# Low parts of a projection's weights by an accumulating DMA in place of a GpSimd subtraction

## The chip, the cores and the metric

The kernel runs on one core of one Trainium2 chip, as one launch. The metric is the device time of that launch in microseconds (us). A core has five engines that run their own instruction streams and wait for each other by semaphores: PE (TensorE, matmuls; its weight loads are listed as PEld), DVE (VectorE), ACT (ScalarE), POOL (GpSimd) and SP (SyncE, which here only issues DMAs). DMAs issued by SP and by POOL move data between HBM and SBUF, or within SBUF.

## The reference, cut to what matters

The reference is a two-layer decoder trunk on 512 tokens of width 1024, all in float32. The piece that the change touches is the first step of layer 1's attention (multi-head latent attention):

```python
def mla_mixer(x, w_down, q_norm, kv_norm, w_uq, w_ukv, w_out):
    down = x @ w_down                      # (512 x 1024) @ (1024 x 800)
    cq, ckv, kr = jnp.split(down, [512, 768], axis=-1)
    q = (rms_norm(cq, q_norm) @ w_uq).reshape(bsz, s, 16, 96)
    ...
```

Its input x is the output of layer 0: `x = layer_norm(DN_ALPHA * h + f + e, ln2_g, ln2_b)`, where f is the last product of layer 0's MLP. So the end of an MLP, a layer norm and this projection follow each other.

## The kernel before

Every matmul is made of three: each float32 operand is split into a high part of type fp32r (a copy with conversion) and a low part (the operand minus its high part), and the products high·high, high·low and low·high are summed in PSUM. `split` (L88) does this with a copy on ACT (L89) and a subtraction on DVE, or on POOL where `sub=nc.gpsimd.tensor_sub` is given (L90). `wload` (L92) loads a weight tile `wraw` with a DMA of SP's queue (L98) and splits it, in `pieces` column blocks, into `whi` and `wlo`. There are two buffers each of `wraw`, `whi` and `wlo` for the whole program, so the split of a tile waits until the matmuls of the tile before the last have read their buffer. A scheduler orders the instructions of each engine at build time; `ahead` raises the priority of a split in it.

Activations stand transposed: eight row tiles `y0` to `y7` of 128 features x 512 tokens. The stretch around the change has these steps:

- Layer 0's last MLP product adds its column tiles into `y4` to `y7` (DVE, L884). The last two, `y6` and `y7`, are made in two halves of 256 tokens (`tail=1`).
- The layer norm (class `Norm`, `onepass`) sums as the tiles come: DVE adds `y` into `n_s1` (L245), ACT squares `y` into `n_sq` (L256), DVE adds that into `n_s2` (L257). For each token half, PE then turns the sums into columns (L274), DVE and ACT make mean and inverse deviation (`n_m`, `n_d`; L277 to L283), PE spreads them (L288), and DVE and ACT make the scaled rows and their parts `hh` and `hl` (L318, L319, L327, L328). POOL makes `y` ready for the next residual (L330).
- PE's stream is in order, and the scheduler has put these small matmuls between those of other work: the first half's L274 stands among the MLP's last matmuls (L107 to L109), the second half's among those of the projection.
- `group_n` (L905) is the projection. Its weights are `w_dn0` (query, 512 columns) and `w_dn1` (key/value, 288 columns). Each has two weight tiles ("chunk 0" and "chunk 1" in what follows), and each chunk has four row tiles k, split one by one (`pieces=4`). For tokens 0 to 255 PE goes through k = 0 to 7 (L916 with `whi`, L917 with `wlo`, L918 with `hl`, for two token blocks each, so six matmuls for a k), then for tokens 256 to 511 again. So chunk 0 serves k = 0 to 3 and chunk 1 k = 4 to 7. The low parts of all of them are made on POOL.

Of the kernel before, what the change touches and what calls it, by code (L numbers as in the profile page):

```python
# [12 lines left out]
OP = mybir.AluOpType  # L13
# [40 lines left out]
def hybrid_kernel(ctx: ExitStack, tc: tile.TileContext, a: dict, out: bass.AP):  # L54
    nc = tc.nc
    uid = [0]

    def nm(s):
        uid[0] += 1
        return f"{s}_{uid[0]}"  # L60
# [9 lines left out]
    def f(ap):  # L70
        return ap.bitcast(F32)
# [7 lines left out]
    def ps_tile(tag=None):  # L79
        if tag is None:  # L80
            tag = TURN[turn[0] % 6]
            turn[0] += 1
        return psum.tile([P, S], F32, tag=tag, bufs=BANKS[tag], name=nm("ps"))
# [4 lines left out]
    def split(hi, lo, src, act=None, sub=None):  # L88
        (act or nc.scalar.copy)(hi, src)  # L89
        (sub or nc.vector.tensor_sub)(lo, src, f(hi))  # L90

    def wload(dram, idx, n=2048, pieces=2, sub=None, raw=None, ahead=30):  # L92

        hi = wp.tile([P, 2048], F32R, tag="whi", name=nm("whi"))
        lo = wp.tile([P, 2048], F32R, tag="wlo", name=nm("wlo"))
        if raw is None:
            raw = wp.tile([P, 2048], F32, tag="wraw", name=nm("wraw"))
            nc.sync.dma_start(raw[:, :n], dram[idx, :, :n])  # L98
        m = n // pieces
        with tc.high_priority(ahead):  # L100
            for i in range(pieces):
                c = slice(i * m, (i + 1) * m)
                split(hi[:, c], lo[:, c], raw[:, c], sub=sub)
        return hi, lo

    def mm3(ps, whi, wlo, xhi, xlo, start, stop):
        nc.tensor.matmul(ps, whi, xhi, start=start, stop=False)  # L107
        nc.tensor.matmul(ps, whi, xlo, start=False, stop=False)  # L108
        nc.tensor.matmul(ps, wlo, xhi, start=False, stop=stop)  # L109
# [1 line left out]
    ALL, HALVES = slice(0, S), (slice(0, H), slice(H, S))  # L111

    def gemm_t(dram, idxs, xs, evac, kk=8, nt=2, lead=0, ps=ps_tile, sub=None, loaded=None,
               halves=(), tail=0, ahead=30):

        tiles = {}  # L120

        def part(g, c, w, kn, cs=ALL):
            ktot = kk * len(idxs[g])
            for k, n in kn:
                key = g, n, cs.start
                if key not in tiles:
                    tiles[key] = ps()
                kx = c * kk + k
                hi, lo = xs[kx]
                o = slice((k * nt + n) * P, (k * nt + n + 1) * P)  # L130
                mm3(tiles[key][:, cs], w[0][:, o], w[1][:, o], hi[:, cs], lo[:, cs],
                    kx == 0, kx == ktot - 1)
                if kx == ktot - 1:
                    evac(g * nt + n, tiles[key], cs)

        first, last = 0, len(idxs) - tail
        byn = [(k, n) for n in range(nt) for k in range(kk)]
        byk = [(k, n) for k in range(kk) for n in range(nt)]
        if lead:
            w = loaded or [wload(dram, idxs[g][0], sub=sub, ahead=ahead) for g in range(2)]  # L140
            first = 2
            for cs in HALVES if "lead" in halves else (ALL,):
                for k in range(lead):
                    for g in range(2):
                        part(g, 0, w[g], [(k, n) for n in range(nt)], cs)
                for g in range(2):
                    kn = (byk, byn)[g]
                    part(g, 0, w[g], [t for t in kn if t[0] >= lead], cs)
        for g in range(first, last):
            for c, idx in enumerate(idxs[g]):  # L150
                part(g, c, wload(dram, idx, sub=sub, ahead=ahead), byn)
        if tail:
            w = {(g, c): wload(dram, idx, sub=sub, ahead=ahead) for g in range(last, len(idxs)) for c, idx in enumerate(idxs[g])}
            for cs in HALVES:
                for g in range(last, len(idxs)):
                    cn = [(c, n) for n in range(nt) for c in range(len(idxs[g]))]
                    for c, n in cn if cs.start == 0 else sorted(cn):
                        part(g, c, w[g, c], [(k, n) for k in range(kk)], cs)
# [12 lines left out]
    for k in range(KT):  # L171
        c = slice(k * 256, (k + 1) * 256)
# [283 lines left out]
    def mixer0(mixed):  # L456
        with pool("m0", 1) as m0, pool("m0s") as sc:
# [58 lines left out]

            kt = []
            gemm_t(a["w_in"], [[1], [0]], x, ev0, lead=8, loaded=w0)


# [139 lines left out]

            rcs = []
            gemm_t(a["w_in"], [[2], [3]], x, ev1, sub=nc.gpsimd.tensor_sub)
            topk()
            gemm_full([4, 5], ev2)
# [58 lines left out]
    def out_proj(dram, idxs, xs, norm, **kw):  # L723
        def ev(n, ps, cs):
            yn = y[n][:, cs]
            nc.vector.tensor_add(yn, yn, ps[:, cs])
            if n == 3:
                norm.first()
            elif n > 3:
                norm.add(n, cs)  # L730


        first = iter((ps_g, ps_g))
        gemm_t(dram, idxs, xs, ev, ps=lambda: next(first, ps_tile)(), **kw)
# [165 lines left out]
    def mixer1(x1, mixed):  # L900
        with pool("m1", 1) as m1, ExitStack() as pools:
            cst_ = ExitStack()
            cp = cst_.enter_context(pool("m1c"))

            def group_n(dram, ncols, xs, evac):  # L905

                ps = [ps_tile() for _ in range(NB)]
                w = [[u[:, :4 * ncols].rearrange("p (k n) -> p k n", n=ncols)
                      for u in wload(dram, ci, 4 * ncols, pieces=4, sub=nc.gpsimd.tensor_sub)] for ci in range(2)]
                for half in range(2):  # L910
                    for k in range(KT):
                        for b in (2 * half, 2 * half + 1):
                            c = slice(b * P, (b + 1) * P)
                            o = ps[b][:, :ncols]
                            (hi, lo), (whi, wlo) = xs[k], (u[:, k % 4] for u in w[k // 4])
                            nc.tensor.matmul(o, hi[:, c], whi, start=k == 0, stop=False)  # L916
                            nc.tensor.matmul(o, hi[:, c], wlo, start=False, stop=False)  # L917
                            nc.tensor.matmul(o, lo[:, c], whi, start=False, stop=k == KT - 1)  # L918
                    for b in (2 * half, 2 * half + 1):
                        evac(b, ps[b])  # L920
# [12 lines left out]
            def transposed(src, n, col, tag):  # L933

                o = []
                for i in range(n):
                    pt = ps_tile()
                    for b in range(NB):
                        nc.tensor.transpose(pt[:, b * P:(b + 1) * P], src[b][:, i * P:(i + 1) * P], ident)
                    g = small[:, col + i:col + i + 1]  # L940
                    hi = m1.tile([P, S], F32R, tag=f"{tag}h{i}", name=nm(tag))
                    lo = m1.tile([P, S], F32R, tag=f"{tag}l{i}", name=nm(tag))
                    nc.scalar.activation(hi, pt, AF.Copy, scale=g)
                    nc.vector.scalar_tensor_tensor(lo, pt, g, f(hi), op0=OP.mult, op1=OP.subtract)
                    o.append((hi, lo))
                return o
# [8 lines left out]
            def ev_kv(b, ps):  # L955
                ckn[b] = rms_scale(ps[:, :256], 256)
                nc.scalar.copy(kr[:, b], ps[:, 256:288])

            group_n(a["w_dn0"], 512, x1, ev_q)
            group_n(a["w_dn1"], 288, x1, ev_kv)  # L960
            cq = transposed(cqn, 4, C_QN, "cq")

            def rope(dst, src, tmp, cs, sn):
# [8 lines left out]
            for b in range(NB):  # L972
                ps = ps_tile()
                c = slice(b * P, (b + 1) * P)
                for k in range(4):
                    hi, lo = cq[k]
# [128 lines left out]
    for layer in range(2):  # L1105
        mixed = [None] * KT
        if layer == 0:
            mixer0(mixed)
        else:
            mixer1(h, mixed)  # L1110
        with pool(f"mlp{layer}") as mp:
            with pool(f"norm{layer}a", 1) as npool:
                norm = Norm(npool, layer, 0)
                if layer == 0:
                    out_proj(a["w_out0"], [[2], [3]], mixed[4:], norm, kk=4, nt=4, tail=1, sub=nc.gpsimd.tensor_sub)
                else:
                    out_proj(a["w_out1"], [[i] for i in range(4)], mixed, norm, lead=7, tail=2)
                pp = embed(layer, mp)
            h = mlp(layer, norm, pp, mp)
# [98 lines left out]
```

## Time and profile before

| | |
|---|---|
| median of 3 runs | 1269.17 us (1267.67 to 1270.79) |
| the profiled execution: its own time | 1267.45 us |
| its span (first to last instruction) | 1265.7 us |
| PE busy | 1225.8 us, 97% of the span |
| DVE busy | 924.4 us, 73% |
| ACT busy | 667.1 us, 53% |
| POOL busy | 167.4 us, 13% |
| mean granted TensorE clock | 0.99 of full speed |

The busy share of PE is that of pipelined matmuls whose ends are modelled, so a busy PE is not a PE at its peak; what counts is where it stood idle, for whom, and at which granted clock it ran. [...] Idle time of an engine that nobody waits for costs nothing. Times of rows are microseconds from the start of the span. One row of a merged view can stand for several instructions in a row (x3), and then its second number is the stretch that they filled together.

### The profile page before, as it was taken

The page shows a single profiled execution, that of the slowest core. Times are in us where ns is not written, and L with a number is a line of the kernel's source. Part 1 is how long each engine was busy: PE and PEld are TensorE (multiplying, and loading weights), DVE is VectorE, ACT ScalarE, POOL GpSimd, SP SyncE. Part 2 cuts the span into 40 slices and gives each one's busy share as a digit, 9 for nine tenths or more (in the row PEclk, how much of TensorE's full clock was granted, in tenths as well). Part 3 has the DMA queues.
Part 4 walks back from the last instruction along what each step waited for, and adds up shares of the span by engine and source line. Part 5 has one row for each costly group of instructions (what it writes and reads, how often), then busy time and mean ns, then how long its engine had stood idle before and what let it go on. Part 6 is the DMA issues. An engine that isn't in the chain of part 4 may idle for free.

```text
span 1265.7 us, 18749 instructions
## 1 busy us (share of the span) xinstructions
PE 1225.8 (97%) x7240; PEld 1063.4 (84%) x7240; DVE 924.4 (73%) x1793; ACT 667.1 (53%) x1216; POOL 167.4 (13%) x202
## 2 busy tenths in 40 slices
PE   8898899999999999999899999999999999999998
PEld 6744678989899898897797888799898998988987
DVE  5998867998566575586838788579985674855857
ACT  4594664656335254364356888446563362542633
POOL 0501660000000000000544553300000000000000
PEclk9998899999999999999999999999999999999999
DMA  6211122122323314123113111122232231231311
GB/s 217 101 33 67 67 76 75 68 101 100 126 75 134 100 67 134 67 101 133 38 68 117 51 51 51 50 85 83 100 134 97 70 133 68 100 134 67 134 34 68
DMA packets 22457, 113.07 MB, mean 89 GB/s; under 512 B 2976, under 2 KB 7072, under 8 KB 10176
## 3 DMA queue, kind: packets, MB, share of 16 engines
q1 hardware_dynamic: 22272, 111.28, 25.6%
q8 instruction: 57, 0.93, 0.3%
q0 software_dynamic: 96, 0.59, 0.2%
q14 instruction: 32, 0.26, 0.1%
HBM read 107.66 MB, written 2.10 MB: 87 GB/s over the span
## 4 chain that ended last, share of the span: by engine, by line
PE 81%; DVE 12%; ACT 3%; issue 1%; POOL 1%; DMA 1%; ACTq 0%; SPq 0%; POOLq 0%; DVEq 0%
PE ps L793 26%; PE ps L107 15%; PE ps L108 15%; PE ps L109 15%; DVE mb L551 2%; DVE m L550 2%; PE ps L397 2%; PE ps L417 1%; ACT whi L89 1%; PE ps L1095 1%; PE ps L917 1%; PE ps L918 1%; PE ps L916 1%; PE ps L1096 1%; DVE xc L611 1%
## 5 line engine op out<-in xcount | busy, mean ns | idle before, releaser
L89 ACT CAST whi<-wraw 128x1024 fp32r<-128x1024 f32 (+3 forms) x154 | 129.9, 882 | 151.2 <-PE ps L108 118.3
L107 PE MATMUL ps<-ah,whi 128*128 128x512 f32 (+1 forms) x544 | 206.4, 379 | 0.0
L108 PE MATMUL ps<-al,whi 128*128 128x512 f32 (+1 forms) x544 | 206.4, 379 | 0.0
L109 PE MATMUL ps<-ah,wlo 128*128 128x512 f32 (+1 forms) x544 | 205.3, 377 | 0.0
L107 PE MATMUL ps<-hh,whi 128*128 128x256 f32 (+1 forms) x432 | 147.1, 343 | 6.7 <-ACT hh L89 5.2
L109 PE MATMUL ps<-hh,wlo 128*128 128x256 f32 (+1 forms) x432 | 145.4, 340 | 1.4 <-DVE wlo L90 0.8
L108 PE MATMUL ps<-hl,whi 128*128 128x256 f32 (+1 forms) x432 | 146.5, 340 | 0.0
L90 POOL TENSOR_TENSOR wlo<-wraw,whi 128x512 fp32r<-128x512 f32 (+2 forms) x46 | 72.8, 1605 | 472.8 <-ACT whi L89 440.3
L90 DVE TENSOR_TENSOR wlo<-wraw,whi 128x1024 fp32r<-128x1024 f32 (+1 forms) x108 | 115.6, 1102 | 19.9 <-ACT whi L89 19.7
L793 PE MATMUL ps<-xt,whi 128*128 128x256 f32 x680 | 124.6, 284 | 0.0
L108 PEld LDWEIGHTS ps<-al,whi 128*128 128x128 f32 x544 | 102.8, 189 | 20.1 <-DVE al L90 1.2
L107 PEld LDWEIGHTS ps<-ah,whi 128*128 128x128 f32 x544 | 102.8, 189 | 19.5 <-ACT ah L89 1.1
L109 PEld LDWEIGHTS ps<-ah,wlo 128*128 128x128 f32 x544 | 102.8, 189 | 18.6 <-issue 0.5
L793 PEld LDWEIGHTS ps<-xt,whi 128*128 128x128 f32 x680 | 106.0, 192 | 0.4
L758 ACT CAST whi<-wraw 128x1024 fp32r<-128x1024 f32 (+1 forms) x43 | 36.0, 837 | 130.8 <-PE ps L108 89.6
L884 DVE TENSOR_TENSOR y<-y,ps 128x512 f32<-128x512 f32 (+1 forms) x52 | 33.3, 644 | 94.7 <-PE ps L109 94.6
L793 PE MATMUL ps<-xt,wlo 128*128 128x256 f32 x340 | 96.2, 283 | 0.0
L107 PEld LDWEIGHTS ps<-hh,whi 128*128 128x128 f32 x432 | 82.7, 192 | 16.1 <-ACT hh L89 5.2
L109 PEld LDWEIGHTS ps<-hh,wlo 128*128 128x128 f32 x432 | 82.5, 192 | 11.3 <-DVE wlo L90 2.0
L108 PEld LDWEIGHTS ps<-hl,whi 128*128 128x128 f32 x432 | 82.9, 192 | 8.7 <-DVE hl L90 0.6
L793 PE MATMUL ps<-hh,wlo 128*128 128x256 f32 x260 | 73.5, 283 | 0.0
L793 PE MATMUL ps<-hl,whi 128*128 128x256 f32 x260 | 73.5, 283 | 0.0
(335 smaller groups left out, 2951.7 us busy)
## 6 DMA issues: line engine op xcount, KB each, us to landing
wraw<-in_mlp_w SPq DMA_DIRECT2D x64, 1024.0 KB, 4.8
wraw<-in_w_out SPq DMA_DIRECT2D x8, 1024.0 KB, 5.1
wraw<-in_w_gate SPq DMA_DIRECT2D x8, 1024.0 KB, 4.7
wraw<-in_w_in SPq DMA_DIRECT2D x6, 1024.0 KB, 4.7
wraw<-in_w_ukv SPq DMA_DIRECT2D x4, 1024.0 KB, 4.7
wraw<-in_w_in SPq DMA_DIRECT2D x16, 128.0 KB, 5.0
y<-in_xT SPq DMA_DIRECT2D x8, 256.0 KB, 3.6
wraw<-in_w_proj SPq DMA_DIRECT2D x2, 1024.0 KB, 4.9
```

What stands on the lines that cost most here:

```text
L89: (act or nc.scalar.copy)(hi, src)
L90: (sub or nc.vector.tensor_sub)(lo, src, f(hi))
L107: nc.tensor.matmul(ps, whi, xhi, start=start, stop=False)
L108: nc.tensor.matmul(ps, whi, xlo, start=False, stop=False)
L109: nc.tensor.matmul(ps, wlo, xhi, start=False, stop=stop)
L397: nc.tensor.transpose(ps[t][:, c:c + P], self.L[blk][:, kb * P:(kb + 1) * P], ident)
L417: nc.tensor.matmul(po[:, c], v, hi, start=kb == 0, stop=kb == NB - 1)
L550: nc.vector.max(out=m8, in_=src)
L551: nc.vector.match_replace(out=w, in_to_replace=m8, in_values=src, imm_value=LOWEST)
L758: nc.scalar.copy(hi, src)
L793: nc.tensor.matmul(o, u[:, c], v, start=start and k == n == 0, stop=k == 3 and n == 2, skip_group_check=True)
L884: nc.vector.tensor_add(yn, yn, ps[:, cs])
```

## The change

For the query part `w_dn0` alone, the four pieces of both chunks are no longer split with a POOL subtraction. ACT copies the piece into `whi` as before, then ACT writes the negated high part into `wlo`, and a DMA issued from POOL's queue adds the raw weights to it in place (`accum_op`). The other weights keep their split; `w_dn1` gets its subtraction named in the call. The scheduler's priority step for these pieces is 60 in place of 30. Six lines come in ahead, so the lines of the kernel after are 6 higher from L107 on (L330 becomes L336, L917 becomes L923).

```diff
-    def wload(dram, idx, n=2048, pieces=2, sub=None, raw=None, ahead=30):
+    def wload(dram, idx, n=2048, pieces=2, sub=None, raw=None, ahead=30, adds=False):
...
         with tc.high_priority(ahead):
             for i in range(pieces):
                 c = slice(i * m, (i + 1) * m)
-                split(hi[:, c], lo[:, c], raw[:, c], sub=sub)
+                if adds:
+                    nc.scalar.copy(hi[:, c], raw[:, c])
+                    nc.scalar.mul(lo[:, c], f(hi[:, c]), -1.0)
+                    nc.gpsimd.dma_start(f(lo[:, c]), raw[:, c], accum_op=OP.add)
+                else:
+                    split(hi[:, c], lo[:, c], raw[:, c], sub=sub)
...
-            def group_n(dram, ncols, xs, evac):
+            def group_n(dram, ncols, xs, evac, **how):
...
-                      for u in wload(dram, ci, 4 * ncols, pieces=4, sub=nc.gpsimd.tensor_sub)] for ci in range(2)]
+                      for u in wload(dram, ci, 4 * ncols, pieces=4, **how)] for ci in range(2)]
...
-            group_n(a["w_dn0"], 512, x1, ev_q)
-            group_n(a["w_dn1"], 288, x1, ev_kv)
+            group_n(a["w_dn0"], 512, x1, ev_q, ahead=60, adds=True)
+            group_n(a["w_dn1"], 288, x1, ev_kv, sub=nc.gpsimd.tensor_sub)
```

POOL's order from the first piece of chunk 0 on, before (`wlo_5857` is chunk 0, `wlo_5869` chunk 1; `y_67` to `y_74` are `y0` to `y7`, first token half):

```order
L90 TENSOR_TENSOR wlo_5857<-wraw_5858,whi_5856 128x512 x4
L330 TENSOR_SCALAR y_67<-y_67,small 128x256
L330 TENSOR_SCALAR y_68<-y_68,small 128x256
L330 TENSOR_SCALAR y_69<-y_69,small 128x256
L90 TENSOR_TENSOR wlo_5869<-wraw_5870,whi_5868 128x512 x2
L330 TENSOR_SCALAR y_70<-y_70,small 128x256
L90 TENSOR_TENSOR wlo_5869<-wraw_5870,whi_5868 128x512
L330 TENSOR_SCALAR y_71<-y_71,small 128x256
L90 TENSOR_TENSOR wlo_5869<-wraw_5870,whi_5868 128x512
```

The same place in the change (`wlo_5873` is chunk 1 now):

```order
L107 DMA wlo_5857<-wraw_5858 128x512 x4
L336 TENSOR_SCALAR y_67<-y_67,small 128x256
L336 TENSOR_SCALAR y_68<-y_68,small 128x256
L336 TENSOR_SCALAR y_69<-y_69,small 128x256
L336 TENSOR_SCALAR y_70<-y_70,small 128x256
L107 DMA wlo_5873<-wraw_5874 128x512
L336 TENSOR_SCALAR y_71<-y_71,small 128x256
L107 DMA wlo_5873<-wraw_5874 128x512 x2
L336 TENSOR_SCALAR y_72<-y_72,small 128x256
L336 TENSOR_SCALAR y_73<-y_73,small 128x256
L107 DMA wlo_5873<-wraw_5874 128x512
```

The eight subtractions are gone, eight DMA issues stand in their place, and the first one of chunk 1 has moved behind the step on `y3` (`y_70`).

ACT's order at chunk 0, before (the squares are those of `y3` to `y6`):

```order
L256 ACTIVATE n_sq_5511<-y_70 128x512
L89 CAST whi_5856<-wraw_5858 128x512 x3
L256 ACTIVATE n_sq_5549<-y_71 128x512
L89 CAST whi_5856<-wraw_5858 128x512
L256 ACTIVATE n_sq_5579<-y_72 128x512
L256 ACTIVATE n_sq_5617<-y_73 128x256
```

And in the change:

```order
L262 ACTIVATE n_sq_5511<-y_70 128x512
L105 CAST whi_5856<-wraw_5858 128x512 x2
L106 ACTIVATE wlo_5857<-whi_5856 128x512
L262 ACTIVATE n_sq_5549<-y_71 128x512
L106 ACTIVATE wlo_5857<-whi_5856 128x512
L262 ACTIVATE n_sq_5579<-y_72 128x512
L105 CAST whi_5856<-wraw_5858 128x512 x2
L106 ACTIVATE wlo_5857<-whi_5856 128x512 x2
L262 ACTIVATE n_sq_5617<-y_73 128x256
```

All eight instructions of chunk 0 now stand ahead of the square of `y6` (`n_sq_5617`), where four stood.

ACT's order at chunk 1, before (`hh` of `y3` to `y7`, first token half, then the square of `y6`, second half):

```order
L89 CAST whi_5868<-wraw_5870 128x512 x2
L327 ACTIVATE hh_5691<-y_70,small 128x256
L327 ACTIVATE hh_5698<-y_71,small 128x256
L89 CAST whi_5868<-wraw_5870 128x512 x2
L327 ACTIVATE hh_5705<-y_72,small 128x256
L327 ACTIVATE hh_5712<-y_73,small 128x256
L327 ACTIVATE hh_5719<-y_74,small 128x256
L256 ACTIVATE n_sq_5751<-y_73 128x256
```

And in the change:

```order
L105 CAST whi_5872<-wraw_5874 128x512 x2
L333 ACTIVATE hh_5691<-y_70,small 128x256
L333 ACTIVATE hh_5698<-y_71,small 128x256
L106 ACTIVATE wlo_5873<-whi_5872 128x512 x2
L105 CAST whi_5872<-wraw_5874 128x512
L333 ACTIVATE hh_5705<-y_72,small 128x256
L106 ACTIVATE wlo_5873<-whi_5872 128x512
L333 ACTIVATE hh_5712<-y_73,small 128x256
L105 CAST whi_5872<-wraw_5874 128x512
L333 ACTIVATE hh_5719<-y_74,small 128x256
L106 ACTIVATE wlo_5873<-whi_5872 128x512
L262 ACTIVATE n_sq_5751<-y_73 128x256
```

The first two negations come behind the `hh` of `y4`, the third behind that of `y5`, the last behind that of `y7`.

## Rows read from the trace of the kernel before

**Rows 1.** The page's chain of work that ended last: shares by engine.

```profile
PE 81%; DVE 12%; ACT 3%; issue 1%; POOL 1%; DMA 1%; ACTq 0%; SPq 0%; POOLq 0%; DVEq 0%
```

**Rows 2.** Waits of PE, whole span: total us, times, longest us.

```profile
PE ps L274 <- DVE n_s L245: 5.1, 2, 3.0
...
PE ps L397 <- POOL l L388: 3.1, 3, 1.8
```

**Rows 3.** Timeline of PE, first token half: start, us, instruction, [idle before <-releaser].

```profile
613.38 0.58 PE L274 MATMUL ps<-cst,n_s 128*128 128x1 f32 x4 [2.96 <-DVE n_s L245]
613.81 0.36 PE L107 MATMUL ps<-ah,whi 128*128 128x256 f32 x1
...
617.56 0.83 PE L288 MATMUL ps<-cst,n_d 128*128 128x128 f32 x4
618.14 0.36 PE L107 MATMUL ps<-ah,whi 128*128 128x256 f32 x1
...
621.46 0.40 PE L916 MATMUL ps<-whi,hh 128*128 128x512 f32 x1
```

**Rows 4.** Timeline of DVE, first token half.

```profile
605.97 1.77 DVE L257 TENSOR_TENSOR n_s<-n_s,n_sq 128x512 f32<-128x512 f32 x1
...
612.80 0.42 DVE L245 TENSOR_TENSOR n_s<-n_s,y 128x256 f32<-128x256 f32 x1
...
619.61 1.27 DVE L328 SCALAR_TENSOR_TENSOR hl<-y,small,hh 128x256 fp32r<-128x256 f32 x3
```

**Rows 5.** Timeline of POOL, both chunks.

```profile
604.20 6.39 POOL L90 TENSOR_TENSOR wlo<-wraw,whi 128x512 fp32r<-128x512 f32 x4 [414.59 <-ACT whi L89]
620.19 1.87 POOL L330 TENSOR_SCALAR y<-y,small 128x256 f32<-128x256 f32 x3 [9.60 <-DVE hl L328]
622.25 2.73 POOL L90 TENSOR_TENSOR wlo<-wraw,whi 128x512 fp32r<-128x512 f32 x2 [0.20 <-ACT whi L89]
```

**Rows 6.** DVE by line, 1233 to 1242 us (layer 1's norm): count | busy us, mean ns.

```profile
L257 DVE TENSOR_TENSOR n_s<-n_s,n_sq 128x512 f32<-128x512 f32 x5 | 3.4, 685 | 0.0
```

**Rows 7.** Timeline of ACT, both chunks and the next weights.

```profile
603.44 1.66 ACT L89 CAST whi<-wraw 128x512 fp32r<-128x512 f32 x3 [2.34 <-PE ps L108]
605.00 0.63 ACT L256 ACTIVATE n_sq<-y 128x512 f32<-128x512 f32 x1
...
621.54 1.15 ACT L89 CAST whi<-wraw 128x512 fp32r<-128x512 f32 x2 [1.29 <-PE ps L108]
622.59 0.90 ACT L327 ACTIVATE hh<-y,small 128x256 fp32r<-128x256 f32 x2
...
645.43 0.77 ACT L89 CAST whi<-wraw 128x288 fp32r<-128x288 f32 x2 [0.85 <-PE ps L918]
```

**Rows 8.** Windows: length, busy of PE PEld DVE ACT POOL, clock, DMA, GB/s.

```profile
614.60:618.10 3.50, 3.50 (x18) 3.50 (x18) 1.62 (x7) 0.20 (x1) 0.00 (x0) 0.51 0.00 0
631.50:638.30 6.80, 6.80 (x25) 6.03 (x26) 2.81 (x10) 0.77 (x3) 0.00 (x0) 0.51 0.01 4
189.70:192.00 2.30, 2.30 (x16) 1.95 (x16) 0.57 (x2) 0.61 (x2) 0.00 (x0) 1.00 0.99 415
```

**Rows 9.** Timeline of PE, second token half's sums among the projection.

```profile
626.93 0.39 PE L916 MATMUL ps<-whi,hh 128*128 128x512 f32 x1
...
631.47 0.81 PE L274 MATMUL ps<-cst,n_s 128*128 128x1 f32 x4 [2.11 <-DVE n_s L245]
...
639.75 0.39 PE L916 MATMUL ps<-whi,hh 128*128 128x512 f32 x1
```

**Rows 10.** Timeline of DVE beside the second chunk.

```profile
623.13 2.14 DVE L328 SCALAR_TENSOR_TENSOR hl<-y,small,hh 128x256 fp32r<-128x256 f32 x2 [0.47 <-ACT hh L327]
```

**Rows 11.** DMA issues: tiles, queue, count, KB each, median us from issue to landing.

```profile
wraw<-in_w_dn SPq DMA_DIRECT2D x2, 576.0 KB, 3.4
...
q<-hl SPq DMA_DIRECT2D x9, 64.0 KB, 2.1
...
kh<-in_aug POOLq DMA_DIRECT2D x1, 64.0 KB, 5.9
```

More of the change, by code (lines that the diff above doesn't have):

```diff
@@ L113, in gemm_t @@
     def gemm_t(dram, idxs, xs, evac, kk=8, nt=2, lead=0, ps=ps_tile, sub=None, loaded=None,
-               halves=(), tail=0, ahead=30):
+               halves=(), tail=0, ahead=30, adds=False):
         tiles = {}
@@ L139, in gemm_t @@
         if lead:
-            w = loaded or [wload(dram, idxs[g][0], sub=sub, ahead=ahead) for g in range(2)]
+            w = loaded or [wload(dram, idxs[g][0], sub=sub, ahead=ahead, adds=adds) for g in range(2)]
             first = 2
@@ L150, in gemm_t @@
             for c, idx in enumerate(idxs[g]):
-                part(g, c, wload(dram, idx, sub=sub, ahead=ahead), byn)
+                part(g, c, wload(dram, idx, sub=sub, ahead=ahead, adds=adds), byn)
         if tail:
-            w = {(g, c): wload(dram, idx, sub=sub, ahead=ahead) for g in range(last, len(idxs)) for c, idx in enumerate(idxs[g])}
+            w = {(g, c): wload(dram, idx, sub=sub, ahead=ahead, adds=adds) for g in range(last, len(idxs)) for c, idx in enumerate(idxs[g])}
             for cs in HALVES:
```

## The prediction

> **What bounds the kernel now.** I read the chain that ended last first: PE holds 81% of it and DVE 12% [rows 1], so what can be gained is where PE waits, and the next view is PE's waits. Over the whole span the matmuls on the norm's sums (L274) waited twice for DVE's additions into `n_s1` (L245), 5.1 us together [rows 2]. PE's timeline puts both beside the changed line: 2.96 us before 613.38 [rows 3], 2.11 us before 631.47 [rows 9]. After each wait the granted clock is 0.51, from 614.6 to 618.1 and from 631.5 to 638.3 [rows 8]; a wait of 1.8 us elsewhere (PE for POOL, L397) [rows 2] is followed by a clock of 1.00 [rows 8].
>
> Why is DVE late? One addition of 128x512 into `n_s2` (L257) takes 1.77 us at 605.97 [rows 4], but 685 ns for each of five in layer 1 [rows 6]. What differs is POOL: from 604.20 it subtracts four pieces for 6.39 us [rows 5], reading SBUF as DVE does. At 623.13, beside the next subtractions [rows 5], two `hl` steps (L328) take 2.14 us [rows 10]; three of them at 619.61 took 1.27 [rows 4], although POOL's L330 ran beside them from 620.19 [rows 5]. So these subtractions slow the chain on which PE waits, and not everything on POOL does.
>
> **What goes: the first token half.** I take everything ahead of 603.44 as unchanged. DVE's two additions into `n_s2` and one into `n_s1` shrink from 1.77 to about 0.6 each (starts of back-to-back 685 ns additions lie 0.6 apart, so I use 0.6), and `y6` could be added at about 607.7. Then ACT is later. It now has eight steps for chunk 0 and two squares before the square of `y6`. A copy costs 0.55 (three in 1.66 us), a square 0.63 [rows 7]; the negation is not in the trace, and I price it at a square's, since both are ACT steps of 128x512 out of SBUF; a copy's price would be the lower bound, a doubled one the upper. Four copies, four negations and two squares at 0.55, 0.6 and 0.6 (back to back, rows overlap a little) are 5.8 us: ACT is free at 609.25. The square of `y6` ends at 609.65; DVE's addition of it, and then those for `y7` (L884, L245), need 0.4 each: 610.9, where this stood at 613.22 [rows 4]. PE starts L274 at 611.0 in place of 613.38: **2.4 us**, with 0.6 of its wait left.
>
> PE then does the same work at full clock. From 613.38 to 618.14 it took 4.76 us [rows 3]: two pairs of sums (L274), 12 small matmuls, two spreads (L288). At full clock a sum step takes 0.43, a spread 0.58 (618.14 less 617.56) [rows 3], a small matmul 0.12: 3.5 us. `n_d` comes about 1.1 us after the second sum step and costs PE 0.1 more waiting. **1.1 us.**
>
> **The second half** (times of before from here on). ACT's copies of chunk 1 can't start before 621.54, when PE releases `whi` [rows 7]. In the new order two copies end at 622.7, `hh` of `y3` and `y4` at 623.5 (0.45 each [rows 7]), negations at 624.1 and 624.65, the third copy at 625.2, `hh` of `y5` at 625.65, the third negation 626.25, then `hh`, copy, `hh`, negation: 628.25. DVE without slowed steps follows: `hl` of `y7` at 628.35, the four additions for `y6` and `y7` up to 629.55. PE gets to L274 at 631.47 less 2.11, 629.36 [rows 9], and starts it at 629.65: **1.8 us**. From there to the first matmul of tokens 256 on took 8.28 us (631.47 to 639.75 [rows 9]); at full clock it is 14 matmuls of 0.228 (24 of them fill 621.46 to 626.93 [rows 3, 9]), two sum steps and two spreads, 5.2 us: **3.1 us**.
>
> **What comes: the DMAs.** Chunk 0 is not urgent: its last DMA can be issued at about 609.3, and k = 3 is used only some 12 us later. In chunk 1 POOL comes to the first DMA behind L330 of `y3`, at 624.25, and PE wants that `wlo` at 627.15 (k = 4, its second matmul [rows 9]). So 2.9 us from issue to landing are free. No transfer here adds into SBUF. Within SBUF 64 KB land in 2.1 us, from HBM 576 KB in 3.4; POOL's queue shows 5.9 for 64 KB, while the loads of the program's start fill the engines [rows 11]. These two, 2.1 and 5.9, are my bounds. A piece is 256 KB, read once as source and once as destination: 512 KB on the line through 64 KB and 576 KB give 3.3 us. I take that, nearer the quiet rows, because no load runs at this moment. PE then waits 0.4 us at k = 4 and loses the 0.3 before L274: **0.1 us back**. The next three pieces are issued 1.3, 2 and 4 us after the first and are wanted 1.4, about 4 and about 6 after.
>
> [...]
>
> Does issuing a DMA slow DVE as a subtraction does? No row shows POOL issuing beside DVE. At worst the second half would gain nothing, 4.9 us. I take zero: L330 did not slow `hl` [rows 4, 5]. [...]
>
> The `wraw` of chunk 0 comes free when its last DMA lands, some 2 us later than before, and SP's load of `w_dn1` behind it (3.4 us [rows 11]) starts later; its copies stand at 645.43 [rows 7], so 25 us hide this. SP holds nothing else in between.
>
> **Sum.** 2.4 + 1.1 + 1.8 + 3.1 − 0.1 = 8.3 us. Against the profiled execution's own 1267.45 (span 1265.7) this is 1259.2. The median of the runs is 1.7 above that execution: **1260.9 us**.
>
> **Rivals.**
> *The DMA is late enough to cost the clock.* At 5.9 us from issue to landing PE waits 3.0 at k = 4, more than the 2.11 after which the clock fell. The stretch at 0.51 was 3.5 and 6.8 us long, and costs 1.2 to 3.1 by the two stretches above. Of 8.3, 2.6 to 4.5 remain: 1264.6 to 1266.6. For it: POOL's only rows. Against: those lie in the busiest stretch of DMA.
> *Adding in a DMA is slow, and the pieces go one after another.* With d us a piece, the last of chunk 1 lands at 624.25 + 4d, and PE wants it at about 633: it waits 4d − 9, with the clock lost too. It breaks even where this wait is 6.5, at d = 3.9; at d = 5 it waits 11 and the time is 1273.7, slower. Against: 576 KB load in 3.4 [rows 11], so d = 5 would be a third of that rate. For: no row shows an addition.
> *The change frees nothing, because ACT takes POOL's place.* At double the price (1.26) the negations end chunk 0 at 611.8, L245 at 613.4, and `hh` of `y7` comes 1.9 later in the second half: both waits stay, 1268 to 1269.5, within 0.3%. Against: no ACT step of this width and kind costs that. An issue that slows DVE belongs here with half the effect.
>
> **How the numbers follow.** 0.3%, about what a measurement can tell from no change, is 3.8 us. Forecast 0.64: with landings between 2.1 and 4.7 us (a wait of 1.8, still at full clock) the gain is 8.4 to 6.9, and with the spread of the median its own range is 1259.3 to 1263.8. Late DMA 0.17, half of it over 3.8. Slow adding 0.11, nearly all slower. ACT 0.08, same. Faster: 0.64 + 0.085 = 0.72; same: 0.085 + 0.08 + 0.01 = 0.18; slower 0.10. The range 1258.5 to 1267.5 leaves out the last two cases, 0.19.
>
> **What would show it.** L257 at 0.69 us each beside chunk 0; PE's wait at L274 under 1 us in both places; a clock of 1.00 from 614 to 640; the wait of L923 (L917 of before) for the first DMA of chunk 1 under 2 us; from `w_dn1` on every row some 8 us earlier, otherwise alike. Wrong: landings over 5 us, a wait at L923 with a clock of 0.5 behind it, L257 still over 1 us, or `n_sq` of `y6` after 611.

## The result

The changed kernel takes 1259.44 us (median of 4 runs, 1258.99 to 1259.88), the kernel before on the same chip 1268.42 (median of 4). The ratio is 0.9929, 95% interval [0.9915, 0.9944]: faster by 9.0 us or 0.7%. All times in this document are of fast executions; one of the run with doubled DMAs below, 2002.09 us at a granted clock of 0.557, is left out. The change's profiled execution has a span of 1258.1 us at a mean clock of 0.993 (before: 1265.7 at 0.990).

The page first: the busy line (section 1) and the line of POOL's DMA queue (section 3: packets, MB, share of 16 engines), the latter then once more as it was before.

```profile
PE 1223.4 (97%) x7240; PEld 1060.1 (84%) x7240; DVE 920.1 (73%) x1793; ACT 671.4 (53%) x1224; POOL 163.1 (13%) x202
...
q0 software_dynamic: 1248, 2.69, 1.1%
...
q0 software_dynamic: 96, 0.59, 0.2%
```

Eight steps more on ACT, 2.1 MB more on POOL's queue, and shares that hardly move: the page alone doesn't tell where 9 us went. PE's waits over the whole span do (lines are six higher than before: L280 was L274, L923 was L917):

```profile
PE ps L403 <- POOL l L394: 3.1, 3, 1.9
...
PE ps L923 <- DMA wlo<-wraw: 0.2, 1, 0.2
```

The wait of the sums for DVE, 5.1 us in [rows 2], is in no row any more; the one for POOL at L403 stands as it was; the new one, for the adding DMA, is 0.2 us. PE's timeline of both token halves, as in [rows 3] and [rows 9]:

```profile
611.12 0.58 PE L280 MATMUL ps<-cst,n_s 128*128 128x1 f32 x4
...
617.96 0.40 PE L922 MATMUL ps<-whi,hh 128*128 128x512 f32 x1
...
624.04 0.50 PE L923 MATMUL ps<-wlo,hh 128*128 128x512 f32 x1 [0.23 <-DMA wlo<-wraw]
...
626.45 0.58 PE L280 MATMUL ps<-cst,n_s 128*128 128x1 f32 x4
...
631.69 0.39 PE L922 MATMUL ps<-whi,hh 128*128 128x512 f32 x1
```

Neither L280 row lists a wait any more. ACT's timeline has the eight new steps; the first copy of chunk 0 is the row above them, and the square of `y6` the last:

```profile
604.10 1.14 ACT L105 CAST whi<-wraw 128x512 fp32r<-128x512 f32 x2 [2.36 <-PE ps L114]
605.15 0.63 ACT L106 ACTIVATE wlo<-whi 128x512 fp32r<-128x512 f32 x1
605.68 0.61 ACT L262 ACTIVATE n_sq<-y 128x512 f32<-128x512 f32 x1
606.20 0.61 ACT L106 ACTIVATE wlo<-whi 128x512 fp32r<-128x512 f32 x1
...
609.33 0.40 ACT L262 ACTIVATE n_sq<-y 128x256 f32<-128x256 f32 x1
```

These rows give two stages that every run below can be measured by. Stage A goes from ACT's first copy of chunk 0 to the first matmul of the projection (L922), stage B from there to the first of tokens 256 on. Before they are 621.46 − 603.44 = 18.02 us [rows 3, 7] and 639.75 − 621.46 = 18.29 [rows 9]; now 617.96 − 604.10 = 13.86 and 631.69 − 617.96 = 13.73. Together 8.7 us are gone, which is the whole result to within the spread of the runs. The first copy itself starts 0.66 later in this execution; nothing of the change stands ahead of it.

DVE's timeline, the rows that answer to [rows 4] and [rows 10], and two more from the second half:

```profile
606.40 0.68 DVE L263 TENSOR_TENSOR n_s<-n_s,n_sq 128x512 f32<-128x512 f32 x1
...
607.60 0.68 DVE L263 TENSOR_TENSOR n_s<-n_s,n_sq 128x512 f32<-128x512 f32 x1
...
609.76 0.43 DVE L263 TENSOR_TENSOR n_s<-n_s,n_sq 128x256 f32<-128x256 f32 x1 [0.68 <-ACT n_sq L262]
...
619.62 0.88 DVE L334 SCALAR_TENSOR_TENSOR hl<-y,small,hh 128x256 fp32r<-128x256 f32 x2 [0.47 <-ACT hh L333]
...
625.03 0.94 DVE L263 TENSOR_TENSOR n_s<-n_s,n_sq 128x256 f32<-128x256 f32 x1
625.89 0.41 DVE L251 TENSOR_TENSOR n_s<-n_s,y 128x256 f32<-128x256 f32 x1
```

POOL's timeline, as [rows 5], then the landing of the eight DMAs (L107 by itself):

```profile
606.35 1.86 POOL L107 DMA_DIRECT2D wlo<-wraw  x2 [416.40 <-ACT n_sq L262]
609.19 1.74 POOL L107 DMA_DIRECT2D wlo<-wraw  x2 [0.97 <-ACT wlo L106]
...
620.81 0.88 POOL L107 DMA_DIRECT2D wlo<-wraw  x1
...
625.23 1.74 POOL L336 TENSOR_SCALAR y<-y,small 128x256 f32<-128x256 f32 x1
```

```profile
DMA to landing us min/median/max: 3.2/4.0/4.4
```

The long additions of 1.77 us are back at 0.68, and the two `hl` steps beside chunk 1 take 0.88 where they took 2.14 [rows 10]. In chunk 0 DVE runs beside POOL's issues (606.35 to 608.2, 609.19 to 610.9) without a stretched step. In chunk 1, where issues and L336's passes alternate on POOL, one addition of 128x256 takes 0.94 in place of 0.42.

The windows (length, busy time of PE, PEld, DVE, ACT, POOL, granted clock, DMA share, GB/s) have the second part of the gain:

```profile
609.00:612.00 3.00, 2.95 (x25) 2.78 (x24) 1.68 (x5) 1.14 (x3) 1.74 (x2) 1.00 1.01 183
...
612.00:615.00 3.00, 3.00 (x26) 2.80 (x25) 1.69 (x8) 0.20 (x1) 0.00 (x0) 1.00 0.50 90
...
614.00:619.00 5.00, 5.00 (x39) 4.68 (x38) 4.78 (x14) 2.28 (x5) 1.87 (x3) 1.00 0.35 118
...
624.00:627.00 3.00, 2.94 (x14) 2.11 (x15) 2.64 (x6) 0.93 (x3) 2.97 (x4) 1.00 0.94 169
627.00:632.00 5.00, 5.00 (x29) 4.19 (x29) 3.79 (x13) 1.87 (x6) 0.70 (x2) 1.00 0.59 160
...
630.00:640.00 10.00, 10.00 (x46) 8.28 (x45) 9.04 (x24) 7.15 (x19) 5.19 (x9) 1.00 0.17 59
640.00:650.00 10.00, 10.00 (x70) 9.53 (x69) 0.49 (x3) 6.41 (x21) 5.42 (x8) 1.00 0.53 184
```

Behind the sums of both halves (L280, at 611.12 and 626.45) the clock is 1.00; behind the same sums it was 0.51 before [rows 8].

### The profile page after: what moved, and what is told of

It is laid out like the page before. It is cut to its first block, busy times and chain, and to the rows that moved or that the text cites. A ratio compares the mean times of both kernels' runs of the same rounds, so it can differ in the third digit from the quotient of the medians.

```text
span 1258.1 us, 18771 instructions
## 1 busy us (share of the span) xinstructions
PE 1223.4 (97%) x7240; PEld 1060.1 (84%) x7240; DVE 920.1 (73%) x1793; ACT 671.4 (53%) x1224; POOL 163.1 (13%) x202
## 3 DMA queue, kind: packets, MB, share of 16 engines
q0 software_dynamic: 1248, 2.69, 1.1%
## 4 chain that ended last, share of the span: by engine, by line
PE 81%; DVE 12%; ACT 3%; DMA 1%; issue 1%; POOL 1%; SPq 0%; ACTq 0%; POOLq 0%; DVEq 0%
PE ps L799 25%; PE ps L115 15%; PE ps L113 15%; PE ps L114 15%; DVE mb L557 2%; DVE m L556 2%; PE ps L403 2%; PE ps L423 1%; PE ps L1101 1%; PE ps L923 1%; PE ps L924 1%; PE ps L922 1%; PE ps L1102 1%; DVE xc L617 1%; ACT whi L89 1%
## 5 line engine op out<-in xcount | busy, mean ns | idle before, releaser
L89 ACT CAST whi<-wraw 128x1024 fp32r<-128x1024 f32 (+3 forms) x146 | 125.3, 896 | 146.7 <-PE ps L114 114.3
L799 PE MATMUL ps<-hh,whi 128*128 128x256 f32 x260 | 73.4, 283 | 0.0
```

The source lines that it names most:

```text
L799: nc.tensor.matmul(o, u[:, c], v, start=start and k == n == 0, stop=k == 3 and n == 2, skip_group_check=True)
```

## The experiments

The theory: POOL's subtractions hold up DVE's additions into the sums and its `hl` steps (1.77 us for 0.685 [rows 4, 6], 2.14 for two steps [rows 10]); PE waits for these (2.96 and 2.11 us [rows 3, 9]), and each wait is followed by some us at half clock (3.5 and 6.8 us at 0.51 [rows 8]); the adding DMA takes POOL's passes out of DVE's way and lands early enough. Rivals: the new priority step (`ahead=60`) did it; any way of taking the work off POOL is as good; the DMAs have a price that is hidden in the sum; a late DMA would cost what the wait for DVE cost. Each run is timed against the kernel before on its own chip.

| run | median us | ratio, 95% interval | stage A | stage B |
|---|---|---|---|---|
| before | 1268.42 | | 18.02 | 18.29 |
| the change | 1259.44 | 0.9929 [0.9915, 0.9944] | 13.86 | 13.73 |
| priority alone | 1267.62 | 0.9998 [0.9988, 1.0008] | 18.02 | 18.29 |
| adding DMAs, old priority | 1259.13 | 0.9928 [0.9913, 0.9943] | 13.87 | 13.69 |
| chunk 0 alone | 1262.43 | 0.9954 [0.994, 0.9969] | 13.87 | 16.68 |
| chunk 1 alone | 1264.18 | 0.9967 [0.9957, 0.9977] | 18.02 | 13.65 |
| subtraction on DVE | 1261.74 | 0.9956 [0.9944, 0.9968] | 13.50 | 17.18 |
| no DMAs | 1258.06 | 0.9932 [0.9918, 0.9945] | 13.87 | 13.10 |
| POOL subtracts as well | 1266.82 | 0.9996 [0.9988, 1.0005] | 21.45 | 13.70 |
| one-input passes on POOL | 1263.57 | 0.9973 [0.9961, 0.9985] | 17.85 | 13.72 |
| DMAs of chunk 1 twice | 1264.52 | 0.9971 [0.9961, 0.9981] | 13.87 | 19.74 |
| chunk 0 on DVE, chunk 1 by DMA | 1259.38 | 0.9938 [0.9926, 0.995] | 13.51 | 13.93 |
| the change again | 1259.64 | 0.9938 [0.9926, 0.995] | 13.87 | 13.72 |

The stages are read from the same three rows of each run's own profile. Runs of one chip share the kernel before: the four experiments from the priority to chunk 1 alone (1267.91 us), the next four (1267.23), the last three (1268.04).

**Priority or adding.** Two kernels: the subtraction on POOL with the new priority step (the edit is to the kernel before), and the adding DMAs with the old one (this edit, and all that follow, are to the changed kernel).

```diff
-for u in wload(dram, ci, 4 * ncols, pieces=4, sub=nc.gpsimd.tensor_sub)] for ci in range(2)]
+for u in wload(dram, ci, 4 * ncols, pieces=4, sub=nc.gpsimd.tensor_sub, **how)] for ci in range(2)]
...
-group_n(a["w_dn0"], 512, x1, ev_q)
+group_n(a["w_dn0"], 512, x1, ev_q, ahead=60)
```

> The subtraction on POOL is kept; only the scheduler's priority step of these pieces is 60 as in the change. Contention theory (POOL's subtraction slows DVE, on which PE waits): both waits at L274 stay, 2 to 3 us each, and the time stays at that of before, 1268 within 2. Priority theory (the gain comes from the earlier place of the pieces): 1260 to 1262.

```diff
-group_n(a["w_dn0"], 512, x1, ev_q, ahead=60, adds=True)
+group_n(a["w_dn0"], 512, x1, ev_q, adds=True)
```

> The negation and the accumulating DMA are kept, the priority step is back at 30. Contention theory: the time of the change, 1259.4 within 1, both waits at the sums gone. Priority theory: nearer to 1268.

The first is the kernel before in its time and in PE's waits:

```profile
PE ps L274 <- DVE n_s L245: 5.1, 2, 3.0
```

The second is the changed kernel in both (its only new wait is 0.2 us for `wlo`). The priority step does nothing by itself and nothing for the change; that rival falls.

**One chunk at a time.** The other chunk keeps its subtraction on POOL.

```diff
-for u in wload(dram, ci, 4 * ncols, pieces=4, **how)] for ci in range(2)]
+for u in wload(dram, ci, 4 * ncols, pieces=4, **(how if ncols < 512 or ci == 0 else dict(ahead=60, sub=nc.gpsimd.tensor_sub)))] for ci in range(2)]
```

> Accumulating DMA for chunk 0 alone, POOL's subtraction for chunk 1. Contention theory: the first wait and its stretch at half clock go, the second pair stays: 4 us faster than before (3.5 by the forecast's first two terms, 4.2 by the profile after), about 1264.3. If the gain sat in one place alone: either 1259 or 1268.

With `ci == 1` in its place:

> Accumulating DMA for chunk 1 alone, POOL's subtraction for chunk 0. Contention theory: the second wait and its stretch at half clock go, the first pair stays: 4.6 to 4.8 us faster than before, about 1263.7; the two halves add up to the whole change. If the gain sat in one place alone: either 1259 or 1268.

PE's waits for the sums, chunk 0 alone and then chunk 1 alone:

```profile
PE ps L280 <- DVE n_s L251: 2.1, 1, 2.1
```

```profile
PE ps L280 <- DVE n_s L251: 3.0, 1, 3.0
```

Each leaves the wait of the half that keeps its subtractions, at the size it had in [rows 9] and [rows 3]. By their medians the two gains are 5.5 and 3.7 us against the before of that chip (1267.91), where 4 and 4.6 to 4.8 were expected; together they are 9.2, and the whole change gives 9.0. By the stages they don't add up: chunk 0 alone takes 4.15 us from stage A and 1.6 from stage B, chunk 1 alone 4.6 from stage B, and these are 10.4 where the whole change has 8.7. So the two halves overlap in stage B. What they share is the clock: with chunk 0 alone, the stretch at half clock after the wait of 2.1 us is some 3.3 us long, and it was 6.8 before [rows 8] (the clock is the number before the last two):

```profile
629.50:632.80 3.30, 3.30 (x13) 2.98 (x12) 1.79 (x7) 0.25 (x2) 0.00 (x0) 0.50 0.03 7
```

The same wait does not always cost the same clock.

**Is it the DMA, or only that POOL is idle?** The subtraction goes to DVE (`sub` not named).

```diff
-group_n(a["w_dn0"], 512, x1, ev_q, ahead=60, adds=True)
+group_n(a["w_dn0"], 512, x1, ev_q, ahead=60)
```

> The low parts of the query weights by subtraction on DVE itself, nothing on POOL or by DMA. Contention theory: no step of DVE is stretched, but eight subtractions of 0.7 us stand in its own queue, some of them ahead of the sums and the low parts that PE needs: the first wait is under 1.5 us, PE waits 1 to 2 us for the low parts of chunk 1, and the time lies between, 1261 to 1265. Rival (what costs before is POOL's lateness with the low parts, not DVE's stretching): no gain, since DVE is later still, 1268 to 1270.

```profile
PE ps L923 <- DVE wlo L90: 2.5, 1, 2.5
```

The sums wait no more, and stage A is even 0.4 shorter than with the change. But in chunk 1 DVE has `hl` and the norm's additions of the second half to do first, and PE waits 2.5 us for a low part (1 to 2 were expected); stage B gains only 1.1. So POOL's being out of the way is what counts in chunk 0, and in chunk 1 the work has to be off DVE as well.

**What do the DMAs cost?** The line that issues them is taken out, so that `wlo` holds only the negated high part: the low parts are missing from what is computed.

> The change without its eight DMAs, so the low parts of these weights are the negated high parts (this part of the computation is left out). Contention theory with the small price of the DMAs: 0.2 to 0.6 us faster than the change, about 1259, no wait for low parts at k = 4. Rival (issuing and landing cost more than the one wait shows, through DVE or PE): 1 us or more faster than the change, 1258 or less.

PE's first product of the projection and its sums of the second token half, then DVE's addition that these sums wait for:

```profile
617.03 0.40 PE L921 MATMUL ps<-whi,hh 128*128 128x512 f32 x1
...
624.88 0.58 PE L279 MATMUL ps<-cst,n_s 128*128 128x1 f32 x4
```

```profile
624.12 0.61 DVE L250 TENSOR_TENSOR n_s<-n_s,y 128x256 f32<-128x256 f32 x1
```

Stage A is the same to 0.01 us, stage B 0.63 shorter. All of it lies ahead of the second half's sums: they start 7.85 us after the first product, and 8.49 with the DMAs (626.45 − 617.96). The sums follow DVE's last addition into `n_s1` by 0.15 us in both (it ends at 624.73 here, at 626.30 with the DMAs), so what the DMAs cost is that DVE is 0.64 later; the wait of 0.23 for `wlo` is hidden by that. The ratio, 0.9932, does not differ from that of the change (0.9929 and 0.9938): by these two profiles the price is some 0.6 us, more than the 0.1 of the sum, and less than the runs can show.

**Put POOL's passes back.** Everything of the change stays, but in chunk 0 POOL subtracts in place, `wraw` minus `whi`, while ACT writes zeros into `wlo` and the DMA adds the difference to them. (`adds` is 2 for chunk 0 and 1 for chunk 1 here and in the next run; the line that sets it is not shown.)

```diff
-nc.scalar.mul(lo[:, c], f(hi[:, c]), -1.0)
+nc.scalar.mul(lo[:, c], f(hi[:, c]), 0.0 if adds > 1 else -1.0)
+if adds > 1:
+    nc.gpsimd.tensor_sub(raw[:, c], raw[:, c], f(hi[:, c]))
```

> The change, but for chunk 0 POOL also subtracts the high part from the raw weights in place (two inputs from SBUF, 1.3 us a piece), ACT writes zeros in place of negated high parts, and the DMA adds the difference to them. Chunk 0's low parts have 10 us to spare, so its DMAs stay free. Contention theory: DVE's additions beside it take 1.8 us again, the first wait and its half clock are back, 4 us slower than the change, about 1263.5. Rival (the DMA path or ACT's new order made the gain): 1259.4 as the change.

Waits of PE, then the timelines of DVE and POOL:

```profile
PE ps L282 <- DVE n_s L253: 4.5, 1, 4.5
```

```profile
606.75 1.78 DVE L265 TENSOR_TENSOR n_s<-n_s,n_sq 128x512 f32<-128x512 f32 x1
608.46 4.41 DVE L253 TENSOR_TENSOR n_s<-n_s,y 128x512 f32<-128x512 f32 x1
612.79 0.68 DVE L265 TENSOR_TENSOR n_s<-n_s,n_sq 128x512 f32<-128x512 f32 x1
```

```profile
607.93 1.84 POOL L109 DMA_DIRECT2D wlo<-wraw  x2
609.15 3.16 POOL L108 TENSOR_TENSOR wraw<-wraw,whi 128x512 f32<-128x512 f32 x2
```

The 1.78 is back, and one addition takes 4.41: it ends at 612.87, 0.56 us after POOL's last pass (612.31), a little less than its own time of 0.68. The next, with POOL done, takes 0.68. Stage A grows by 7.6 us, and nearly all of the gain of both chunks is gone with it. The wait is 4.46 us where the kernel before had 2.96 [rows 3], with that one step ahead of it. The clock adds to it: around this wait it is at half for ten us, where it was 3.5 before [rows 8], and so stage A is longer even than before and the time above the 1263.5 that was expected.

```profile
613.20:623.20 10.00, 7.55 (x35) 7.58 (x36) 5.46 (x18) 1.73 (x5) 0.83 (x1) 0.50 0.47 111
```

**One-input passes.** The prediction took L330, a POOL pass with one input, as harmless. Here chunk 0 has, ahead of each DMA, two passes on POOL that multiply `wraw` by one in place.

```diff
+if adds > 1:
+    for _ in range(2):
+        nc.gpsimd.tensor_scalar(raw[:, c], raw[:, c], 1.0, 1.0, op0=OP.mult, op1=OP.mult)
 nc.gpsimd.dma_start(f(lo[:, c]), raw[:, c], accum_op=OP.add)
```

> The change, but for chunk 0 POOL also passes twice over each piece of raw weights with one input from SBUF (times one, 0.65 us a pass, as long together as a subtraction). If any reading by POOL slows DVE's two-input additions: as with the subtraction, 4 us slower than the change, additions of over 1.2 us. If only a two-input pass does: 1259.4, additions of 0.7 us. The row of the scaling step beside DVE's low parts (not slowed) speaks for the second.

Timelines of DVE and of POOL:

```profile
606.43 1.09 DVE L266 TENSOR_TENSOR n_s<-n_s,n_sq 128x512 f32<-128x512 f32 x1
...
609.93 2.54 DVE L254 TENSOR_TENSOR n_s<-n_s,y 128x256 f32<-128x256 f32 x1
612.40 0.41 DVE L266 TENSOR_TENSOR n_s<-n_s,n_sq 128x256 f32<-128x256 f32 x1
```

```profile
609.18 3.01 POOL L109 TENSOR_SCALAR wraw<-wraw 128x512 f32<-128x512 f32 x4
```

PE waits 2.8 us for DVE again, and stage A is nearly that of before. One-input passes hold DVE's two-input additions too: 1.09 for 0.68, and 2.54 for 0.42, this one again up to 0.28 us after the last pass (612.19). The time is 1263.57, 3.7 us under the before of that chip, so over half of the gain is gone. Beside the bare issues in chunk 0 of the change the same additions took 0.68. Each pass on POOL writes SBUF too; no run here tells its reads from its writes.

**Make the DMA late.** After the four adding DMAs of chunk 1 the same four are issued once more, so that each low part is complete only with the second (`adds` is 2 for chunk 1 here; the low part then holds twice the weight minus the high part: other numbers are computed).

```diff
+for i in range(pieces if adds == 2 else 0):
+    c = slice(i * m, (i + 1) * m)
+    nc.gpsimd.dma_start(f(lo[:, c]), raw[:, c], accum_op=OP.add)
```

> The change, but after the four adding DMAs of row chunk 1 the same four are issued once more, so that each low part there is complete only with its second addition (it then holds twice the weight minus the high part: this changes what is computed). Late-DMA theory (lateness past what is hidden stops TensorE, and the stop costs the clock as well): in the changed kernel the first of these DMAs lands 0.2 us after TensorE wants it, and its repeat is issued behind three others, so TensorE should wait some 4 to 6 us for wlo at the chunk's first low-part product, then show about 0.5 of its clock for some us; 1265 to 1269 us. Rival (a late low part is absorbed, since other products stand between): a wait under 1.5 us and 1259 to 1261 us.

PE's timeline, and a window:

```profile
628.14 1.05 PE L283 MATMUL ps<-cst,n_s 128*128 128x1 f32 x8 [2.26 <-DVE n_s L254]
629.44 0.71 PE L297 MATMUL ps<-cst,n_m 128*128 128x128 f32 x4 [0.25 <-DVE n_m L286]
631.18 0.80 PE L926 MATMUL ps<-wlo,hh 128*128 128x512 f32 x1 [1.03 <-DMA wlo<-wraw]
```

```profile
630.00:640.00 10.00, 8.97 (x31) 7.23 (x30) 5.37 (x15) 2.26 (x7) 3.90 (x6) 0.66 0.76 165
```

The time rises by 4.9 us against the change on the same chip (1264.52 against 1259.64), stage B by 6.0, and the clock falls (0.66 from 630 to 640, 1.00 in the change): a late low part costs time and clock, as the theory says. But not as one wait. In this program the scheduler put the sums ahead of the late products, so PE waits for DVE there first (2.26 us) and then 1.03 for the DMA. DVE is no later than in the change (the sums start 8.3 us after the first product here, 628.14 − 619.80, and 8.5 there): it is PE that comes early, because the products that need `wlo` stand behind. The expected wait of 4 to 6 us for `wlo` is not what was seen, and the time is half a us under the expected 1265 to 1269, though far over the rival's 1259 to 1261.

**A mixture.** Chunk 0 on DVE, where that run was best, and chunk 1 by DMA.

```diff
-for u in wload(dram, ci, 4 * ncols, pieces=4, **how)] for ci in range(2)]
+for u in wload(dram, ci, 4 * ncols, pieces=4, **(how if ncols < 512 or ci == 1 else dict(ahead=60)))] for ci in range(2)]
```

> Row chunk 0 subtracted on VectorE (as in the run with both chunks there, where this chunk made TensorE wait nowhere), row chunk 1 by negation and adding DMA (the run with both there waited 2.5 us for VectorE in this chunk). If what counts is only that no engine that TensorE waits for is held up, the wait of 2.5 us goes back to about 0.2 for the DMA and the time is that of the change within its interval, 1258.5 to 1260. If the eight DMAs themselves cost something (the run without them ended some 1 us before the change), half of it comes back: 1258.0 to 1259.0, and a repeat of the change on the same chip lies 0.5 us or more above it.

> The change itself, once more, as the measure for the two others on this chip: 1258.5 to 1260.5 us, ratio to the kernel before 0.991 to 0.9945. TensorE's wait for wlo at the first low-part product of row chunk 1 between 0 and 0.5 us by every theory; should it differ from 0.2 us by more than 0.5, the landing time of an adding DMA varies between executions more than the earlier runs show.

The mixture and the change are equal, 1259.38 and 1259.64 with the same interval. It waits nowhere for `wlo`; it wins 0.35 in stage A and gives back 0.2 in stage B, where PE now waits 0.5 us for ACT's `hh`. Four DMAs fewer show in no time. No version tried beats the change by more than a run can tell.

## Why the prediction was right

- **What bounds it.** Right. The waits at L274 were the place: with them go 8.7 us of two stages, and each half gives a part when it is changed alone.
- **Why DVE is late.** Right in its main claim: POOL's subtractions put back into the changed kernel bring one addition of 1.78 us, one of 4.41 and the loss back. The side claim was too wide: "not everything on POOL does" rested on one row, L330 beside three `hl` steps [rows 4, 5], and one-input passes of 128x512 do stretch additions. What hung on it in the sum was the zero for DMA issuing. That zero held in the first half (0.68 beside the issues). In the second half, where issues alternate with L336's passes, DVE is 0.64 us later than without the DMAs; how much of it is the issues and how much the passes, no run tells.
- **The first half.** Forecast 3.5 us, measured 18.02 − 13.86 = 4.2. The term that was mis-sized is ACT's: eight steps and two squares at 0.55 to 0.6 were to take 5.8 us; from the first copy to the square of `y6` they took 609.33 − 604.10 = 5.2, as rows of 0.61 start 0.52 apart (605.15, 605.68, 606.20). The negation's price, taken from a square, was right (616 ns, median of eight). So the 0.6 us that were to be left of the wait are not there.
- **The second half.** Forecast 4.9 less 0.1 for the DMA, measured 18.29 − 13.73 = 4.6. Up to the sums, 1.7 were forecast and 1.5 measured (631.47 − 621.46 = 10.01 before, 626.45 − 617.96 = 8.49 now); behind them, 3.1 and 3.0 (8.28 before, 5.24 now). So the clock's part was right. Without the DMAs it is 18.29 − 13.10 = 5.2: their price was some 0.6 in place of 0.1, and the rest gave 0.3 more than its 4.9.
- **The DMA.** From issue to landing 3.2 to 4.4 us, median 4.0, against the 3.3 taken; the bounds 2.1 and 5.9 hold it. The piece that PE waits for is the first of chunk 1, issued at 620.81, and L923 runs on it from 624.04: at most 3.2 us, the least of the eight. That the piece that matters is among the quickest was not forecast, and hides that the median was priced 0.7 too low. The 512 KB counted for a piece, as source and as destination, were an estimate: POOL's queue carries 256 KB more a piece (2.69 − 0.59 = 2.1 MB for the eight).
- **`wraw` and `w_dn1`.** Hidden as argued: no row of PE's waits names `w_dn1`'s tiles, and PE is busy all of 630 to 650, where they are used.
- **The sum.** 8.3 forecast, 8.7 in the two stages, 9.0 between the medians. Of the 1.5 us by which the time came out lower, 0.75 is the kernel before, which is 1268.42 here and 1269.17 in the runs the forecast started from; that half is luck of the sample.
- **The rivals.** Late DMA: the mechanism is real (the doubled DMAs cost 4.9 us), but the lateness is 0.2 us. Serial adding: not at that price. Four pieces are issued within 4.6 us and each lands in 4.4 at most; at the 183 GB/s of full DMA engines a piece of 256 KB takes 1.4 us, where this rival needed 3.9. ACT in POOL's place: the negation costs half of that rival's 1.26.

What stays open: why the stretch at half clock was 6.8 us after one wait of 2.1 and 3.3 after another; whether POOL's reads or its writes hold DVE; and why one addition was held for 4.41 us, over a stretch that begins, by the rows, before POOL's pass does (608.46 against 609.15), while the one ahead of it took 1.78.

## What to carry to other kernels

A helper engine that is busy for 13% of the span can still set the end, if its passes hold the steps of the engine that TensorE waits for: look at the same instruction in a stretch where the helper is idle (0.685 us against 1.77) before asking how busy anyone is. A DMA that adds takes a subtraction off DVE and POOL for the price of a negated copy on ACT (0.6 us a piece), about 4 us of latency and the issue on POOL (0.86 to 1.60 us each; among POOL's passes the DMAs cost DVE some 0.6 us here), so it fits where the result is wanted later than that; where the engine that TensorE waits for has room, a plain subtraction there was as good. Waits that let the clock fall are worth more than themselves (5.1 us of waits, 8.7 us of time), but what the clock adds is the least certain part: after waits of the same length it was at half for 6.8 us here and 3.3 there.

## What was not expected of the hardware

- A DVE addition beside POOL's passes isn't slowed by a fixed factor: the two longest end 0.56 and 0.28 us after POOL's last pass does, a little under their own time, as if POOL's program set their length: 4.41 us for 0.68 and 2.54 for 0.42.
- While they add, the DMA engines are full at a low rate: share 1.01 at 183 GB/s from 609 to 612, where plain loads reach 415 GB/s at 0.99 [rows 8].
- After equal waits of 2.1 us at the same place the granted clock was 0.51 for 6.8 us in the kernel before, and 0.50 for 3.3 us in the run with chunk 0 alone. Around the wait of 4.5 us in the run with POOL's subtractions put back it was 0.50 for ten us.
